# DeltaNet trunk: the triangular solve's diagonal blocks go from 16 to 32 rows, their columns dealt to four partitions

## The chip, the cores and the metric

The kernel runs on one core of one Trainium2 chip. The metric is the device time of one execution in microseconds. Three runs of the kernel before gave 3022.20, 3023.15 and 3023.69, median 3023.15. Engines are named as in the profile: PE is the matrix engine (TensorE), PEld its weight loads, DVE the vector engine, ACT the scalar engine, POOL is GpSimd, SP issues the DMAs.

## The reference, cut to what matters

The whole is a two-layer decoder trunk over 272 tokens (16 meta tokens and 256 others) of width 2048, in float32: a gated DeltaNet layer, then a differential attention layer, each followed by an MLP with squared ReLU. The change touches the DeltaNet layer alone, and in it the triangular solve of each chunk:

```python
decay = jnp.exp(jnp.where(tri_incl, G[..., :, None] - G[..., None, :], -jnp.inf))
kb = kc * bc[..., None]
a_kk = jnp.where(tri_strict, jnp.einsum('bhik,bhjk->bhij', kb, kc) * decay, 0.0)
rhs = jnp.concatenate([vc * bc[..., None], kb * jnp.exp(G)[..., None]], axis=-1)
sol = lax.linalg.triangular_solve(a_kk, rhs, left_side=True, lower=True, unit_diagonal=True)
```

For each head a unit lower triangular matrix I + A has to be applied inversely to a right-hand side; the state S is then carried from chunk to chunk.

## The kernel before, in words

The kernel works with chunks of 128, 128 and 16 tokens (`CH`), not with the reference's 64, and with 32 value heads in 8 batches of 4 (`NB`, `HB`). Nearly all of its time goes into the large products of weights and activations. A weight tile of 128x2048 is loaded by SP into `wraw` (three buffers), cut into two halves of 1024 columns, and each half is split into a rounded part `whi` (ACT, L137) and the rest `wlo` (DVE, L139), three buffers for each. `mm3` (L152, L155, L156) then issues three products for each 128x128 block: 48 for a whole tile. I call such a product of 272 columns a weight product, and half a tile (24 of them) a half-tile.

The DeltaNet layer fills the span from about 50 to 1045 us. For each batch b PE works through four tiles of keys and queries (`keys`), four of values (`values`), four of gates (`gates`) and, for batch b-2, four of the output projection (`gate_out`). The small work of the recurrence is written as Python generators. An object `flow` keeps a clock that each weight product moves on, and resumes a generator when its waiting time has run out, so that the recurrence is dealt out between the weight products. A list scheduler then sets the order on each engine; that order is fixed before the kernel runs. Three things force the flow on: a batch's `values` needs the batch before to have finished its second chunk, `keys` of batch b needs batch b-2 to be done, and `gate_out` needs the batch's own output.

For one batch the recurrence has these steps:

- `products` (from L672): the products of keys with keys and queries (`ps_u`), scaled into `UA` by DVE (L712). The diagonal blocks of `UA` are sent to DRAM (`scr`, L718), eight 16x16 blocks for each head and chunk, and POOL then clears the diagonal blocks in `UA` (`below`, L734).
- `solve` (L737 to L757): the blocks come back as `na`, one block for each partition: 2 chunks x 4 heads x 8 blocks, and 4 for the short chunk, 68 in all. `forward` (L624 to L631) inverts them all at once on DVE by forward substitution: for each row i a product of the rows so far with row i of A (L630) and a sum over them (L631), 15 rows. The inverses go through DRAM (L751, L752) into the block diagonal of `DT` (L755) and into `DT3` (L757).
- `core`, with `merge(c)` (L826 to L858) once for each of the two long chunks. From the inverses of 16-row blocks it makes those of 32-row blocks: POOL picks out the part of A that lies inside the 32-row blocks but outside the 16-row ones (`us`), DVE transposes DT (`e16`, L836), PE multiplies (`ps_e`, L840), ACT copies (`ae`, L842), PE multiplies again (`ps_d`, L846), DVE adds (`d32`, L848). Then DVE transposes the result (`dn`, L850) and PE makes NT from it (`ps_n`, L854; copied by ACT, L856). Each PE step is four products of 128x128 by 128x128 in float32, one for each head.
- `core`, chunk by chunk: from the state S come `ps_ks` and `ps_qs` (L880), from them R (DVE, L884). Three products with NT (`ps_a`, L896) with a copy by ACT (L903) or a sum by DVE (L907, L910) between them solve the rest of the triangle; a product with the inverse (`ps_w`, L916) gives w, and ACT scales it (`ws`, L922). `ps_s` (`ps_s2` in the code, L929) and S (L933, L936) carry the state on, `ps_o` (L941) gives the output, which is normed (squares L951, scaling L966) and transposed (`ps_ot`, L810). Every step waits for the one before. The outputs of `core` on PE have two PSUM banks between them (`psc`).
- `halves` (L979, L980) splits the batch's output for `gate_out`.

For the last batch (b = 7) the waits are shorter (`STEP7`), since its `core` has to be done before the last `gate_out`, the one of batch 7, can begin.

Of the kernel before, what the change touches and what calls it, by code (L numbers as in the profile page):

```python
# [10 lines left out]
F32 = mybir.dt.float32  # L11
# [6 lines left out]
P = 128  # L18
D = 2048
KT = D // P  # L20
HD = D // 2
NM = 16
SEQ = 256
L = SEQ + NM
EPS = 1e-6
# [2 lines left out]
PSM, PSC, PSK = 4, 2, 2  # L28
HB = 4
LAG = 2  # L30
G1 = 9
GB = 4
HOLD = 1
QGAP = 3.0
# [468 lines left out]
def gdn(ctx, tc, a, e):  # L503
# [24 lines left out]
    def work(name):  # L528
        return gt.tile([P, HB, P], F32, tag="g1", name=name, bufs=G1)

# [71 lines left out]
    DT = gc.tile([P, 2, HB, P], F32, name="DT")  # L602
    nc.vector.memset(DT, 0.0)
    DT3 = gc.tile([NM, HB, NM], F32, name="DT3")
    KQ3 = gc.tile([P, 2, 64], F32, name="KQ3")
    nc.vector.memset(KQ3, 0.0)

# [16 lines left out]
    def forward(na, xt):  # L624

        parts, w, n = xt.shape
        tmp = gt.tile([parts, w, n], F32, tag="fw_t", name="fw_t", bufs=1)
        for i in range(1, n):
            b = na[:, None, 0:i + 1, i].broadcast_to([parts, w, i + 1])
            nc.vector.tensor_tensor(tmp[:, :, 0:i + 1], xt[:, :, 0:i + 1], b, ALU.mult)  # L630
            nc.vector.tensor_reduce(xt[:, :, i], tmp[:, :, 0:i + 1], AX.X, ALU.add)  # L631

    def heads(t, b):
        return t[:, :, HB * b:HB * b + HB].rearrange("p c (h r) -> p c h r", r=2)
# [30 lines left out]
    def products(b, g, st):  # L665
        kq, prev = g["kq"], g["prev"]
        while not gated or prev and not prev["laid"]:
            yield 1.0
        nc.vector.tensor_scalar(st, st, 4 * EPS, None, ALU.add)
        rs = rsqrt(st.rearrange("p t c h -> p (t c h)"), "rsg", [P, 12]).rearrange("p (t c h) -> p t c h", t=2, h=2)  # L670
        rq = g["rq"] = gk.tile([P, 3, 2, 2], F32, tag="sc_rq", name="sc_rq", bufs=2)
        negc = gk.tile([P, 3, 2, 2], F32, tag="sc_nc", name="sc_nc", bufs=2)  # L672
        sup = g["sup"] = gk.tile([P, 3, 2, 2], F32, tag="sc_sup", name="sc_sup", bufs=2)
        nk = g["nk"] = gk.tile([P, 3, 2], F32, tag="sc_nk", name="sc_nk", bufs=2)
        r2 = gt.tile([P, 3, 2], F32, tag="r2", name="r2")
        nc.vector.reciprocal(r2, st[:, 0])
# [13 lines left out]
        nc.gpsimd.affine_select(gb[:NM, :, 256:L], gb[:NM, :, 256:L], pattern=[[0, HB], [1, NM]], base=0,  # L690
                                channel_multiplier=-1, compare_op=ALU.is_ge, fill=NEG)
        scr = dram.tile([2, HB, 8, NM, NM], F32, name="scr")
        scr3 = dram.tile([HB, NM, NM], F32, name="scr3")
        UA = g["UA"] = []
        for c, (o, n) in enumerate(CH):
            while prev and prev["chunk"] < min(c, 1):
                yield 1.0
            if c < 2:
                ua = gk.tile([P, HB, 2, P], F32, tag="UA", name="UA", bufs=3)
            else:  # L700
                ua = gk.tile([NM, HB, 2, NM], F32, tag="UA3", name="UA3", bufs=2)
            UA.append(ua)
            for h in range(2):
                pu = psk.tile([P, 512], F32, tag="k", name="ps_u")
                pu_v = pu[:n, 0:2 * n].rearrange("p (t i) -> p t i", t=2)
                nc.tensor.matmul(pu_v, kq[:, h, 0, o:o + n], kq[:, h, :, o:o + n], start=True, stop=True)
                for r in range(2):
                    hv = 2 * h + r
                    dec = gt.tile([P, P], F32, tag="dec", name="dec", bufs=2)
                    nc.scalar.activation(dec[:n, :n], gb[:n, hv, o:o + n], AF.Exp,  # L710
                                         bias=ngG[:n, c, HB * b + hv:HB * b + hv + 1])
                    nc.vector.scalar_tensor_tensor(ua[:, hv], pu_v, negc[:n, c, h, r:r + 1],  # L712
                                                   dec[:n, None, :n].broadcast_to([n, 2, n]), ALU.mult, ALU.mult)
                yield UGAP
            if c < 2:
                for bl in range(8):
                    q = slice(NM * bl, NM * bl + NM)
                    nc.sync.dma_start(scr[c, :, bl].rearrange("h j i -> j h i"), ua[q, :, 0, q])  # L718
                below(ua, NM)
            else:  # L720
                nc.sync.dma_start(scr3.rearrange("h j i -> j h i"), ua[:, :, 0, :])
        g["laid"] = True
        while prev and not prev["free"]:
            yield 1.0
        solve(scr, scr3)
        yield STEP7[2] if b == NB - 1 else SOLVE
        while g["values"] < HB:
            yield 1.0
        yield from core(b, g)
# [6 lines left out]

    def solve(scr, scr3):  # L737

        nb = 2 * HB * 8
        na = gt.tile([nb + HB, NM, NM], F32, tag="na", name="na", bufs=1)  # L740
        xt = gt.tile([nb + HB, NM, NM], F32, tag="xt", name="xt", bufs=1)
        diag = lambda t: t.rearrange("p j i -> p (j i)")[:, 0:NM * NM:NM + 1]
        nc.gpsimd.memset(xt, 0.0)
        nc.gpsimd.memset(diag(xt), 1.0)
        nc.sync.dma_start(na[:nb], scr.rearrange("c h b j i -> (c h b) j i"))
        nc.sync.dma_start(na[nb:], scr3)
        nc.vector.memset(diag(na), 1.0)
        forward(na, xt)
        scr2 = dram.tile([nb, NM, NM], F32, name="scr2")
        scr4 = dram.tile([HB, NM, NM], F32, name="scr4")  # L750
        nc.sync.dma_start(scr2, xt[:nb])  # L751
        nc.sync.dma_start(scr4, xt[nb:])  # L752
        for bl in range(8):
            q = slice(NM * bl, NM * bl + NM)
            nc.sync.dma_start(DT[q, :, :, q].rearrange("p c h j -> p (c h) j"),  # L755
                              scr2.rearrange("(x b) m j -> b m x j", b=8)[bl])
        nc.sync.dma_start(DT3, scr4.rearrange("h m j -> m h j"))  # L757

    def values(b, g):

# [34 lines left out]
    def core(b, g):  # L795
# [28 lines left out]
        def flat(t):  # L824
            return t.rearrange("p h j -> p (h j)")

        def merge(c):

            us = work("us")
            nc.gpsimd.affine_select(us.rearrange("p h (b i) -> p h b i", i=32),  # L830
                                    UA[c][:, :, 0, :].rearrange("p h (b i) -> p h b i", i=32),
                                    pattern=[[0, HB], [-32, 4], [0, 32]], base=0, channel_multiplier=1,
                                    compare_op=ALU.is_ge, fill=0.0)
            below(UA[c], 32)
            e16 = work("e16")
            nc.vector.transpose(flat(e16), flat(DT[:, c]))  # L836
            yield step
            _, pE = bank("ps_e")
            for hv in range(HB):
                nc.tensor.matmul(pE[:, hv], us[:, hv], e16[:, hv], start=True, stop=True)  # L840
            ae = work("ae")
            nc.scalar.copy(ae, pE)  # L842
            yield step
            _, pD = bank("ps_d")
            for hv in range(HB):
                nc.tensor.matmul(pD[:, hv], ae[:, hv], DT[:, c, hv], start=True, stop=True)  # L846
            d32 = work("d32")
            nc.vector.tensor_tensor(d32, DT[:, c], pD, ALU.add)  # L848
            dn = work("dn")
            nc.vector.transpose(flat(dn), flat(d32))  # L850
# [427 lines left out]
```

## Time and profile before

| | |
|---|---|
| profiled execution, its own time | 3024.88 us |
| its span, first to last instruction | 3023.1 us |
| median of the three runs | 3023.15 us |
| mean granted PE clock | 0.993 |
| busy over the span | PE 99%, DVE 64%, ACT 49%, POOL 7% |
| DeltaNet stretch (50 to 1045 us) | 995 us, DVE busy 715.90, ACT busy 556.67 |

The profiled execution is 1.73 us above the median, of which 1.78 lie outside the span. A row of a group of instructions gives the line, the engine, what is written from what, the shape, the count after the x, then the total busy time in us and the mean of one instruction in ns, then the time that the engine sat idle before them and what ended it. One product in float32 is recorded as two PE instructions, so that x128 stands for 64 products; digits at the end of a name are dropped (`e16` is e, `d32` is d, `ps_s2` is ps_s); records of one engine overlap, so what a matmul takes of PE is read from the distance between starts.

### The profile page before, as it was taken

What the parts mean: (1) busy time and instruction counts of PE and PEld (TensorE: products, weight loads), DVE (VectorE), ACT (ScalarE), POOL (GpSimd) and SP (SyncE); (2) the same over time, 40 slices, a digit from 0 to 9 for tenths busy, and PEclk for the clock granted to TensorE, in tenths of its full rate; (3) what the DMA queues carried; (4) which work ended last, traced back from release to release, by engine and by line L of the source; (5) the groups of instructions that cost most, each with busy time, mean ns of one, the idle gap of its engine ahead of it and who ended that gap; (6) DMA issues with size and microseconds to landing.
All of it is one profiled execution on the core that took longest, in us unless ns stands there. A gap on an engine that the chain in (4) does not pass through costs nothing. (4 is left out here: it accounts for less than half of the span.)

```text
span 3023.1 us, 57162 instructions
## 1 busy us (share of the span) xinstructions
PE 2981.0 (99%) x23747; PEld 2924.3 (97%) x23747; DVE 1943.6 (64%) x3452; ACT 1490.1 (49%) x2735; POOL 205.2 (7%) x208
## 2 busy tenths in 40 slices
PE   8999999999999899999999999999999999999998
PEld 8999999999999799999999999999999999999998
DVE  7777576776867674555555558777757555555555
ACT  4565555465555454444344434455555444444443
POOL 0100010000100220000000004300004000000001
PEclk9999999999999899999999999999999999999999
DMA  5433343434434444454544443433354555555553
GB/s 211 151 137 122 142 151 135 156 124 153 146 120 144 153 155 180 168 180 169 179 170 176 173 176 145 153 140 138 143 194 165 184 187 190 183 193 183 191 187 112
DMA packets 92468, 488.36 MB, mean 162 GB/s; under 512 B 29104, under 2 KB 32528, under 8 KB 34736
## 3 DMA queue, kind: packets, MB, share of 16 engines
q1 hardware_dynamic: 92208, 484.70, 44.6%
q8 instruction: 187, 3.06, 0.4%
q14 instruction: 73, 0.60, 0.1%
HBM read 481.41 MB, written 3.25 MB: 160 GB/s over the span
## 5 line engine op out<-in xcount | busy, mean ns | idle before, releaser
L139 DVE TENSOR_TENSOR wlo<-wraw,whi 128x1024 fp32r<-128x1024 f32 x872 | 1070.0, 1229 | 770.8 <-ACT whi L137 769.5
L137 ACT ACTIVATE whi<-wraw 128x1024 fp32r<-128x1024 f32 x890 | 940.2, 1059 | 1145.7 <-PE ps_dn L156 432.1
L152 PE MATMUL ps_dn<-yh,whi 128*128 128x272 f32 (+1 forms) x2048 | 583.2, 285 | 0.0
L152 PE MATMUL ps_up<-xh,whi 128*128 128x272 f32 (+1 forms) x2048 | 582.8, 285 | 0.0
L156 PE MATMUL ps_dn<-yl,whi 128*128 128x272 f32 (+1 forms) x2048 | 582.3, 284 | 0.0
L155 PE MATMUL ps_up<-xh,wlo 128*128 128x272 f32 (+1 forms) x2048 | 581.0, 285 | 0.2 <-DVE wlo L139 0.2
L155 PE MATMUL ps_dn<-yh,wlo 128*128 128x272 f32 (+1 forms) x2048 | 580.9, 284 | 0.0
L156 PE MATMUL ps_up<-xl,whi 128*128 128x272 f32 (+1 forms) x2048 | 580.3, 285 | 0.1
L152 PE MATMUL ps_in<-xh,whi 128*128 128x272 f32 x1520 | 460.2, 303 | 0.0
L156 PE MATMUL ps_in<-xl,whi 128*128 128x272 f32 x1520 | 441.6, 291 | 0.8 <-DVE xl L320 0.8
L155 PE MATMUL ps_in<-xh,wlo 128*128 128x272 f32 x1520 | 441.3, 291 | 0.0
L152 PEld LDWEIGHTS ps_up<-xh,whi 128*128 128x128 f32 x2048 | 385.9, 188 | 0.5 <-ACT xh L401 0.4
L155 PEld LDWEIGHTS ps_dn<-yh,wlo 128*128 128x128 f32 x2048 | 386.0, 188 | 0.0
L152 PEld LDWEIGHTS ps_dn<-yh,whi 128*128 128x128 f32 x2048 | 385.5, 188 | 0.0
L156 PEld LDWEIGHTS ps_up<-xl,whi 128*128 128x128 f32 x2048 | 384.8, 188 | 0.5 <-DVE xl L409 0.5
L155 PEld LDWEIGHTS ps_up<-xh,wlo 128*128 128x128 f32 x2048 | 384.6, 188 | 0.5 <-DVE wlo L139 0.5
L156 PEld LDWEIGHTS ps_dn<-yl,whi 128*128 128x128 f32 x2048 | 384.8, 188 | 0.0
L152 PEld LDWEIGHTS ps_in<-xh,whi 128*128 128x128 f32 x1520 | 287.2, 189 | 7.7 <-issue 4.9
L155 PEld LDWEIGHTS ps_in<-xh,wlo 128*128 128x128 f32 x1520 | 287.6, 189 | 1.6 <-issue 0.4
L156 PEld LDWEIGHTS ps_in<-xl,whi 128*128 128x128 f32 x1520 | 286.6, 189 | 1.4 <-DVE xl L320 1.0
L475 DVE TENSOR_TENSOR acc<-acc,ps_dn 128x272 f32<-128x272 f32 (+1 forms) x224 | 95.9, 428 | 122.1 <-PE ps_dn L156 121.4
L152 PE MATMUL ps_at<-xh,whi 128*128 128x272 f32 x512 | 154.5, 302 | 0.0
(313 smaller groups left out, 4476.9 us busy)
## 6 DMA issues: line engine op xcount, KB each, us to landing
wraw<-w_up SPq DMA_DIRECT2D x128, 1024.0 KB, 4.8
wraw<-w_down SPq DMA_DIRECT2D x128, 1024.0 KB, 4.8
wraw<-w_in SPq DMA_DIRECT2D x97, 1024.0 KB, 4.8
wraw<-w_out SPq DMA_DIRECT2D x32, 1024.0 KB, 4.9
wraw<-w_kv SPq DMA_DIRECT2D x32, 1024.0 KB, 4.8
wraw<-w_q SPq DMA_DIRECT2D x16, 1024.0 KB, 5.8
wraw<-w_o SPq DMA_DIRECT2D x16, 1024.0 KB, 5.6
gb<-g_dram SPq DMA_DIRECT2D x8, 544.0 KB, 5.6
```

The lines of the kernel that those rows point to most:

```text
L137: nc.scalar.activation(hi, part, AF.Copy)
L139: inst = eng.tensor_tensor(lo, part, hi.bitcast(F32), ALU.subtract)
L152: one = nc.tensor.matmul(ps, wh, rh, start=(k == 0), stop=False)
L155: nc.tensor.matmul(ps, wl, rh, start=False, stop=False)
L156: ring["mm"] = nc.tensor.matmul(ps, wh, rl, start=False, stop=(k == nk - 1))
L475: nc.vector.tensor_tensor(acc[:, m, :N], acc[:, m, :N], ps[:, :N], ALU.add)
```

## The change

- Blocks of 32 rows (`NS`) go to DRAM in place of those of 16: four DMAs for each long chunk in place of eight, and POOL clears 32-row blocks in `UA` right away.
- There are 2 x 4 x 4 = 32 such blocks. Each is loaded into four partitions, so that all 128 are used, and partition q of the four solves the columns q, q + 4, q + 8, ... of the inverse, eight of them. Since column j is zero above row j, row i works on i // 4 + 1 columns only. `xt` starts with ones on its diagonal, put there by four copies on ACT.
- The short chunk has a `forward` of its own: 4 x 16 partitions, one column each, 15 rows.
- `forward` is now a generator that yields 3.0 units of the flow's clock after each 8 rows; before, it ran in one piece.
- The inverses go back to DRAM in four DMAs, one for each q, and into `DT` in four DMAs in place of eight.
- `merge` keeps only its last part: the transpose `dn` now reads `DT` itself, then `ps_n` and NT. `us`, `e16`, `ps_e`, `ae`, `ps_d` and `d32` are gone, two of its yields too, and `ps_w` reads `DT` in place of `d32`.
- The pool of working tiles has 7 buffers in place of 9 (`G1`).

```diff
-G1 = 9
+G1 = 7
...
+    e4 = gc.tile([P, 4], F32, name="e4")
+    nc.vector.tensor_reduce(e4, ident.rearrange("p (q x) -> p q x", q=4), AX.X, ALU.add)
...
+    def forward(na, xt, w, per, name):
+
+        parts, n = na.shape[0], na.shape[1]
+        tmp = gt.tile([parts, w, n], F32, tag=name, name=name, bufs=1)
         for i in range(1, n):
-            b = na[:, None, 0:i + 1, i].broadcast_to([parts, w, i + 1])
-            nc.vector.tensor_tensor(tmp[:, :, 0:i + 1], xt[:, :, 0:i + 1], b, ALU.mult)
-            nc.vector.tensor_reduce(xt[:, :, i], tmp[:, :, 0:i + 1], AX.X, ALU.add)
+            k = min(w, i // per + 1)
+            b = na[:, None, 0:i + 1, i].broadcast_to([parts, k, i + 1])
+            nc.vector.tensor_tensor(tmp[:, :k, 0:i + 1], xt[:, :k, 0:i + 1], b, ALU.mult)
+            nc.vector.tensor_reduce(xt[:, :k, i], tmp[:, :k, 0:i + 1], AX.X, ALU.add)
+            if i % RUN == RUN - 1:
+                yield RUNGAP
...
-        solve(scr, scr3)
+        yield from solve(scr, scr3)
...
-        forward(na, xt)
-        scr2 = dram.tile([nb, NM, NM], F32, name="scr2")
-        nc.sync.dma_start(scr2, xt[:nb])
+        yield from forward(na, xt, NS // 4, 4, "fw_t")
+        scr2 = dram.tile([P // 4, NS, NS], F32, name="scr2")
+        for q, cols in enumerate(scr2.rearrange("x (s q) j -> q x s j", q=4)):
+            nc.sync.dma_start(cols, xt[P // 4 * q:P // 4 * (q + 1)])
+        yield from forward(ns, xs, 1, NM, "fw_s")
...
         def merge(c):
 
-            us = work("us")
...
-            e16 = work("e16")
-            nc.vector.transpose(flat(e16), flat(DT[:, c]))
-            yield step
-            _, pE = bank("ps_e")
-            for hv in range(HB):
-                nc.tensor.matmul(pE[:, hv], us[:, hv], e16[:, hv], start=True, stop=True)
-            ae = work("ae")
-            nc.scalar.copy(ae, pE)
-            yield step
-            _, pD = bank("ps_d")
-            for hv in range(HB):
-                nc.tensor.matmul(pD[:, hv], ae[:, hv], DT[:, c, hv], start=True, stop=True)
-            d32 = work("d32")
-            nc.vector.tensor_tensor(d32, DT[:, c], pD, ALU.add)
             dn = work("dn")
-            nc.vector.transpose(flat(dn), flat(d32))
+            nc.vector.transpose(flat(dn), flat(DT[:, c]))
             yield step
             _, pN = bank("ps_n")
             ...
-            merged[c] = d32, NT
+            merged[c] = DT[:, c], NT
```

The order on PE at the end of the DeltaNet layer, before: from batch 7's `ps_s` of its second chunk to the first product of its short chunk. The rows with `ps_out` are weight products of the output projection of batch 6; after them none is left until batch 7 is done.

```order
L929 MATMUL ps_s_12158<-ws,kn 128x256 x2
L941 MATMUL ps_o<-w,UA 128x128 x4
L152 MATMUL ps_out<-oh,whi 128x272
L155 MATMUL ps_out<-oh,wlo 128x272
L156 MATMUL ps_out<-ol,whi 128x272
...
L880 MATMUL ps_ks<-S,KQ_262 48x256 x2
L916 MATMUL ps_w<-R,DT_261 16x128 x4
```

The same place now, from the last weight product of batch 6 on.

```order
L159 MATMUL ps_out<-ol,whi 128x272
L927 MATMUL ps_s_12276<-ws,kn 128x256 x2
L939 MATMUL ps_o<-w,UA 128x128 x4
L878 MATMUL ps_ks<-S,kq 128x256 x2
L878 MATMUL ps_qs<-S,kq 128x256 x2
L894 MATMUL ps_a<-R,NT 128x128 x4
L828 MATMUL ps_ot<-ident,ov 128x128 x4
L894 MATMUL ps_a<-t_12328,NT 128x128 x4
L894 MATMUL ps_a<-z,NT 128x128 x4
L914 MATMUL ps_w<-z,DT 128x128 x4
L927 MATMUL ps_s_12361<-ws,kn 128x256 x2
L939 MATMUL ps_o<-w,UA 128x128 x4
```

What moved: the first chunk's last steps and the whole second chunk of batch 7 now come behind the last weight product of batch 6; before, only the short chunk did.

The order on DVE in the middle of a batch's forward substitution, before: one stretch from one `wlo` to the next, with `fw_t` the products of the rows.

```order
L139 TENSOR_TENSOR wlo<-wraw,whi 128x1024
L630 TENSOR_TENSOR fw_t<-xt,na 68x16x11
L792 SCALAR_TENSOR_TENSOR oT<-zt,ps_in 128x272
L631 TENSOR_REDUCE xt<-fw_t 68x16
L959 TENSOR_TENSOR o_ms<-o_ms,sc_rq 128x12
L630 TENSOR_TENSOR fw_t<-xt,na 68x16x12
L960 TENSOR_TENSOR o_ms<-o_ms,sc_rq 128x12
L631 TENSOR_REDUCE xt<-fw_t 68x16
```

The same stretch of a batch now; `fw_s` belongs to the short chunk's forward.

```order
L142 TENSOR_TENSOR wlo<-wraw,whi 128x1024
L639 TENSOR_TENSOR fw_t<-xt,na 128x4x14
L810 SCALAR_TENSOR_TENSOR oT<-zt,ps_in 128x272
L640 TENSOR_REDUCE xt<-fw_t 128x4
L640 TENSOR_REDUCE xs<-fw_s 64x1
L957 TENSOR_TENSOR o_ms<-o_ms,sc_rq 128x12
L639 TENSOR_TENSOR fw_t<-xt,na 128x4x15
L958 TENSOR_TENSOR o_ms<-o_ms,sc_rq 128x12
L639 TENSOR_TENSOR fw_s<-xs,ns 64x12
L640 TENSOR_REDUCE xt<-fw_t 128x4
L959 TENSOR_SCALAR o_ms<-o_ms 128x12
L640 TENSOR_REDUCE xs<-fw_s 64x1
```

What moved: the two forwards are interleaved, each instruction is smaller, and there are more of them. From its first row to its last, a batch's forward lies beside 5 instructions `wlo` before (7 for the last batch) and beside 9 to 13 now.

The order on PE in the second chunk of a middle batch now; before, 24 to 27 weight products stand between one `ps_a` and the next.

```order
L894 MATMUL ps_a<-R,NT 128x128 x4
L789 MATMUL ps_v<-ident,vt 128x128 x2
L789 MATMUL ps_v<-ident,vt 16x128
L155 MATMUL ps_in<-xh,whi 128x272
L158 MATMUL ps_in<-xh,wlo 128x272
L159 MATMUL ps_in<-xl,whi 128x272
...
L894 MATMUL ps_a<-t_6423,NT 128x128 x4
```

What moved: the second chunk of a middle batch is reached later and is then run through faster, with six weight products and the transposes of one value head between these two steps.

More of the change, by code (lines that the diff above doesn't have):

```diff
@@ L22 @@
 NM = 16
+NS = 32
+NBL = P // NS
+RUN, RUNGAP = 8, 3.0
 SEQ = 256
@@ L604, in gdn @@
     DT3 = gc.tile([NM, HB, NM], F32, name="DT3")
+    eye_s = gc.tile([HB * NM, NM], F32, name="eye_s")
+    e4 = gc.tile([P, 4], F32, name="e4")
+    nc.vector.tensor_reduce(e4, ident.rearrange("p (q x) -> p q x", q=4), AX.X, ALU.add)
+    nc.vector.tensor_reduce(eye_s, ident[:HB * NM, :HB * NM].rearrange("p (h j) -> p j h", j=NM), AX.X, ALU.add)
     KQ3 = gc.tile([P, 2, 64], F32, name="KQ3")
@@ L622, in conv_silu @@
         nc.vector.scalar_tensor_tensor(out, th, 1.0, ac, ALU.add, ALU.mult)
-    def forward(na, xt):
-        parts, w, n = xt.shape
-        tmp = gt.tile([parts, w, n], F32, tag="fw_t", name="fw_t", bufs=1)
+    def forward(na, xt, w, per, name):
+        parts, n = na.shape[0], na.shape[1]
+        tmp = gt.tile([parts, w, n], F32, tag=name, name=name, bufs=1)
         for i in range(1, n):
-            b = na[:, None, 0:i + 1, i].broadcast_to([parts, w, i + 1])
-            nc.vector.tensor_tensor(tmp[:, :, 0:i + 1], xt[:, :, 0:i + 1], b, ALU.mult)
-            nc.vector.tensor_reduce(xt[:, :, i], tmp[:, :, 0:i + 1], AX.X, ALU.add)
+            k = min(w, i // per + 1)
[4 more added lines that the diff above has]
+                yield RUNGAP
     def heads(t, b):
@@ L691, in products @@
                                 channel_multiplier=-1, compare_op=ALU.is_ge, fill=NEG)
-        scr = dram.tile([2, HB, 8, NM, NM], F32, name="scr")
+        scr = dram.tile([2, HB, NBL, NS, NS], F32, name="scr")
         scr3 = dram.tile([HB, NM, NM], F32, name="scr3")
@@ L715, in products @@
             if c < 2:
-                for bl in range(8):
-                    q = slice(NM * bl, NM * bl + NM)
+                for bl in range(NBL):
+                    q = slice(NS * bl, NS * bl + NS)
                     nc.sync.dma_start(scr[c, :, bl].rearrange("h j i -> j h i"), ua[q, :, 0, q])
-                below(ua, NM)
+                below(ua, NS)
             else:
@@ L737, in solve @@
     def solve(scr, scr3):
[L739 to L742, printed above, removed]
-        nc.gpsimd.memset(xt, 0.0)
[L744 to L747, printed above, removed]
@@ L748, in solve @@
-        forward(na, xt)
-        scr2 = dram.tile([nb, NM, NM], F32, name="scr2")
-        scr4 = dram.tile([HB, NM, NM], F32, name="scr4")
-        nc.sync.dma_start(scr2, xt[:nb])
-        nc.sync.dma_start(scr4, xt[nb:])
-        for bl in range(8):
-            q = slice(NM * bl, NM * bl + NM)
+        na = gt.tile([P, NS, NS], F32, tag="na", name="na", bufs=1)
+        ns = gt.tile([HB * NM, NM, NM], F32, tag="ns", name="ns", bufs=1)
+        xt = gt.tile([P, NS // 4, NS], F32, tag="xt", name="xt", bufs=1)
@@ new lines, in solve @@
+        xs = gt.tile([HB * NM, 1, NM], F32, tag="xs", name="xs", bufs=1)
+        flat = lambda t: t.rearrange("p j i -> p (j i)")
+        nc.gpsimd.memset(xt, 0.0)
+        for r in range(4):
+            nc.scalar.copy(flat(xt)[:, r:r + (NS + 4) * (NS // 4 - 1) + 1:NS + 4], e4[:, r:r + 1].broadcast_to([P, NS // 4]))
+        nc.scalar.copy(xs[:, 0], eye_s)
+        blocks = scr.rearrange("c h b j i -> (c h b) (j i)")
+        nc.sync.dma_start(flat(na), blocks[None, :, :].broadcast_to([4, P // 4, NS * NS]))
@@ new lines, in solve @@
+        nc.sync.dma_start(flat(ns), scr3.rearrange("h j i -> h (j i)")[:, None, :].broadcast_to([HB, NM, NM * NM]))
+        nc.vector.memset(flat(na)[:, 0:NS * NS:NS + 1], 1.0)
+        nc.vector.memset(flat(ns)[:, 0:NM * NM:NM + 1], 1.0)
+        yield from forward(na, xt, NS // 4, 4, "fw_t")
+        scr2 = dram.tile([P // 4, NS, NS], F32, name="scr2")
+        for q, cols in enumerate(scr2.rearrange("x (s q) j -> q x s j", q=4)):
+            nc.sync.dma_start(cols, xt[P // 4 * q:P // 4 * (q + 1)])
@@ L755, in solve @@
+        yield from forward(ns, xs, 1, NM, "fw_s")
+        scr4 = dram.tile([HB * NM, NM], F32, name="scr4")
+        nc.sync.dma_start(scr4, xs[:, 0])
+        for bl in range(NBL):
+            q = slice(NS * bl, NS * bl + NS)
             nc.sync.dma_start(DT[q, :, :, q].rearrange("p c h j -> p (c h) j"),
-                              scr2.rearrange("(x b) m j -> b m x j", b=8)[bl])
-        nc.sync.dma_start(DT3, scr4.rearrange("h m j -> m h j"))
+                              scr2.rearrange("(x b) m j -> b m x j", b=NBL)[bl])
@@ L759, in values @@
+        nc.sync.dma_start(DT3, scr4.rearrange("(h m) j -> m h j", m=NM))
     def values(b, g):
```

5 lines of the change are left out of this document (removed).

## The prediction

> **What bounds the kernel now.** I read first the page's busy times, then the windows that cut out the DeltaNet layer, the only stage that the change touches, then the waits of PE.
>
> ```profile
> PE 2981.0 (99%) x23747; PEld 2924.3 (97%) x23747; DVE 1943.6 (64%) x3452; ACT 1490.1 (49%) x2735; POOL 205.2 (7%) x208
> ```
>
> ```profile
> 50.00:1045.00 995.00, 983.31 (x7641) 949.69 (x7641) 715.90 (x1548) 556.67 (x1332) 69.83 (x82) 0.99 0.40 140
> 790.00:800.00 10.00, 10.00 (x82) 9.98 (x81) 9.93 (x32) 5.66 (x16) 0.00 (x0) 1.00 0.47 158
> 820.00:830.00 10.00, 10.00 (x82) 10.00 (x82) 6.36 (x11) 4.02 (x4) 0.00 (x0) 1.00 0.37 129
> ```
>
> The columns of the windows are the length, then the busy time of PE, PEld, DVE, ACT and POOL, then the granted clock. In the layer PE is busy for 983.31 of 995 us, DVE for 715.90. Two windows matter later: while a batch's forward substitution runs (790 to 800) DVE is busy for 9.93 of 10 us and PE still never stops; without one (820 to 830) DVE needs 6.36.
>
> ```profile
> PE ps_in L305 <- DVE xg L297: 8.4, 1, 8.4
> PE ps_ot L810 <- ACT ov L966: 6.8, 2, 5.5
> ...
> PE ps_w L916 <- ACT ps_o L951: 1.7, 1, 1.7
> ```
>
> The 8.4 us lie at the kernel's start; the two others lie at the end of the layer, where the last batch's short chunk runs with nothing beside it. So PE sets the time, and a change is worth what it takes from PE's own work, less what it opens as new gaps.
>
> **What goes from PE.** The change removes `ps_e` and `ps_d`: two groups of four float32 products for each of 16 chunk-and-batch pairs, 32 groups.
>
> ```profile
> L846 PE MATMUL ps_d<-DT,ae 128*128 128x128 f32 x128 | 16.9, 275 | 0.0
> L840 PE MATMUL ps_e<-e,us 128*128 128x128 f32 x128 | 16.9, 275 | 0.0
> ```
>
> Here is what one group takes, on PE's timeline:
>
> ```profile
> 969.74 0.29 PE L155 MATMUL ps_out<-oh,wlo 128*128 128x272 f32 x1
> 969.87 0.29 PE L156 MATMUL ps_out<-ol,whi 128*128 128x272 f32 x1
> 969.99 1.05 PE L840 MATMUL ps_e<-e,us 128*128 128x128 f32 x8
> 970.88 1.06 PE L896 MATMUL ps_a<-z,NT 128*128 128x128 f32 x8
> ```
>
> The busy sums give 33.8 us, but records overlap. From the start of `ps_e` to the next start is 0.89 us; a weight product takes 0.126 us in the same way. So 32 x 0.89 = 28.5 us leave PE's work, and this I take. PE waited 0.0 us before either group, so no wait goes with them. The ACT copies, the DVE sums and transposes and POOL's selections that go too lay beside PE's work and are worth nothing by themselves.
>
> **What DVE gets.** A forward now has 31 rows, and the short chunk's own has 15: 46 products and 46 sums for each batch in place of 15 and 15.
>
> ```profile
> L630 DVE TENSOR_TENSOR fw_t<-xt,na 68x256 f32<-68x256 f32 x8 | 4.9, 614 | 0.1
> L630 DVE TENSOR_TENSOR fw_t<-xt,na 68x112 f32<-68x112 f32 x8 | 2.8, 348 | 0.2
> L631 DVE TENSOR_REDUCE xt<-fw_t 68x16 f32<-68x256 f32 x8 | 3.3, 414 | 0.1
> L631 DVE TENSOR_REDUCE xt<-fw_t 68x16 f32<-68x112 f32 x8 | 2.1, 258 | 0.1
> ```
>
> ```profile
> L630 DVE TENSOR_TENSOR fw_t<-xt,na 68x32 f32<-68x32 f32 (+14 forms) x120 | 53.8, 448 | 2.3
> L631 DVE TENSOR_REDUCE xt<-fw_t 68x16 f32<-68x32 f32 (+14 forms) x120 | 35.5, 296 | 1.7
> L850 DVE STREAM_TRANSPOSE dn<-d 128x512 f32<-128x512 f32 x16 | 11.3, 707 | 0.3
> L836 DVE STREAM_TRANSPOSE e<-DT 128x512 f32<-128x512 f32 x16 | 11.3, 705 | 1.9 <-DMA DT<-scr 1.9
> L848 DVE TENSOR_TENSOR d<-DT,ps_d 128x512 f32<-128x512 f32 x16 | 10.9, 683 | 4.3 <-PE ps_d L846 4.0
> ```
>
> From the two sizes of each: a product of n elements takes 141 + 1.85 n ns, a sum 137 + 1.08 n. Row i works on (i // 4 + 1)(i + 1) elements, 3047 over the 31 rows; the short chunk adds 135. That makes 12.4 us of products and 9.7 of sums, 22.1 us a batch; before it was (53.8 + 35.5) / 8 = 11.2. Over 8 batches DVE gains 88 us and loses 22.2 (`e16`, `d32`): 716 + 66 = 782 us of some 980, 80%. As a mean that is no bound. Locally it is close.
>
> ```profile
> wraw<-w_in SPq DMA_DIRECT2D x97, 1024.0 KB, 4.8
> wraw<-w_out SPq DMA_DIRECT2D x32, 1024.0 KB, 4.9
> ```
>
> The layer has 97 + 32 weight tiles, so a half-tile lasts 995 / 258 = 3.86 us on average, and the order puts about 11 of them beside a forward: 42 us. In these DVE has 0.636 x 42 = 27 us of other work and 22.1 of forward: 49 us by durations, 17% too much. But the same sum before is 5 half-tiles, 19 us, against 12.1 + 11.2 = 23.3, 23% too much, and PE lost nothing, since neighbouring records overlap.
>
> What the slack is: a half-tile's `whi` can start when PE leaves the third half-tile before it, 2 x 24 x 0.126 = 6.0 us ahead of its use.
>
> ```profile
> L139 DVE TENSOR_TENSOR wlo<-wraw,whi 128x1024 fp32r<-128x1024 f32 x872 | 1070.0, 1229 | 770.8 <-ACT whi L137 769.5
> L137 ACT ACTIVATE whi<-wraw 128x1024 fp32r<-128x1024 f32 x890 | 940.2, 1059 | 1145.7 <-PE ps_dn L156 432.1
> ```
>
> Less 1.06 and 1.23 that is 3.7 us by which DVE may be late. The new waits lie there too: `dn` now waits for `DT` straight from its DMA, with the next `wlo` queued behind it on DVE and PE behind that; on SP the four stores of the inverses wait for the last sum, with loads of `wraw` behind them. Bounds for all this: 0, or 8 x (7 - 3.7) = 26 us if the 7 us of overload count in full. I take 4, near the lower end, since the heavier-booked stretch before cost nothing.
>
> The Trainium skill ("VectorE: DVE Perf Modes", section on the TRN2 errata) speaks against this part: each vector instruction pays a fixed latency, so many small ones should be avoided. The fits agree (141 and 137 ns, over half of the 22.1 us). By its 151 cycles and one element a cycle the forward would be an estimated 21 us, and the sum would not move.
>
> **What the last batch loses.** Behind batch 6's last weight product PE now has `ps_s` to `ps_o` of batch 7's two chunks, with nothing between. The steps, from these rows (ACT's, then DVE's):
>
> ```profile
> L951 ACT ACTIVATE ps_o<-ov 128x128 f32<-128x128 f32 (+1 forms) x96 | 25.9, 270 | 7.5 <-DVE ov L947 6.3
> L922 ACT ACTIVATE ws<-ps_w,sc_sup 128x128 f32<-128x128 f32 x64 | 19.0, 365 | 13.2 <-PE ps_w L916 13.2
> L951 ACT ACTIVATION_READ_ACCUMULATOR ps_o<-ov 128x1 f32 (+1 forms) x96 | 18.0, 187 | 0.0
> L903 ACT COPY t<-ps_a 128x512 f32<-128x512 f32 x16 | 9.3, 581 | 7.5 <-PE ps_a L896 7.5
> L933 ACT COPY S<-ps_s 128x512 f32<-128x512 f32 x8 | 4.7, 586 | 1.4 <-PE ps_s L929 1.4
> ```
>
> ```profile
> L910 DVE TENSOR_TENSOR z<-z,ps_a 128x512 f32<-128x512 f32 x16 | 10.9, 682 | 10.3 <-PE ps_a L896 10.3
> L884 DVE SCALAR_TENSOR_TENSOR R<-ps_ks,neG,nv 128x128 f32<-128x128 f32 x32 | 9.7, 343 | 2.2 <-PE ps_ks L880 2.2
> L936 DVE SCALAR_TENSOR_TENSOR S<-S,eGL,ps_s 128x128 f32<-128x128 f32 x32 | 9.4, 340 | 9.1 <-PE ps_s L929 9.0
> ```
>
> A group ends 1.05 us after its start. `ps_s` and the copy of S take 1.7; `ps_ks` and four R 2.4; three `ps_a`, each with a copy or a sum and some 0.1 to 0.2 for the hand-overs, 3 x 1.85; `ps_w` and four `ws` 2.4; `ps_s` and four S 2.4: 14.4 us. Two waits may come on top, both estimates: `ps_qs` needs the PSUM bank into which the first chunk's squares are written, four of 0.27 + 0.19 after the copy of `ps_o`, some 1.2 us; and `ps_ot` stands ahead of the second `ps_a`, so its norm and the four scalings come first, some 1.7. So 14.4 to 17.3 us pass, of which PE works 10 x 0.89 + 0.6 = 9.5 that it had to do anyway: 4.9 to 7.8 us of new gaps. Then the clock:
>
> ```profile
> 1004.00:1006.00 2.00, 0.30 (x2) 0.00 (x0) 1.70 (x4) 1.90 (x9) 0.00 (x0) 1.00 0.49 205
> 1006.00:1007.00 1.00, 0.95 (x7) 0.59 (x8) 0.97 (x7) 0.14 (x1) 0.00 (x0) 0.76 0.00 0
> 1007.00:1020.00 13.00, 5.49 (x19) 1.98 (x17) 4.74 (x25) 5.55 (x20) 0.00 (x0) 0.50 0.01 1
> ```
>
> At this place before, after 2 us with 0.30 us of work and the wait of 1.7 us above, PE's clock fell to half and stayed there. Half clock adds 0.89 to each step's group: 0 if it holds, 7 if it falls at once, 3 if midway. I take 7 + 3 = 10 us.
>
> **Smaller edits.** In the middle batches the second chunk runs with six weight products and one head's transposes between two `ps_a`: 0.89 + 6 x 0.126 = 1.65 us and the transposes, where a step needs 1.85. 1 us in all, from 0 to 19 (below). The five small ACT copies replace two `ae` copies; SP issues 21 DMAs a batch for 30; the broadcast load of `na` adds 0.5 MB to a batch's 16 tiles of 1 MB on DMA engines 40% busy; POOL, busy for 70 of 995 us, loses work. Fewer working tiles serve fewer users. All this lies beside PE's work: nothing, and up to 1 us if one of them is late once.
>
> **The sum.** -28.5 + 10 + 4 + 1 = -13.5 us. The profiled execution's 3024.88 (span 3023.1 and 1.8 around it) becomes 3011.4; it stood 1.7 above the median, so 3009.6 for the median.
>
> **The rivals.**
>
> *All hidden* (0.12): the last batch costs its lower bound 5, the rest nothing: 3023.15 - 23.5 = 2999.6. For it: DVE's overload cost nothing before. Against it: the order leaves the chain bare.
>
> *The clock falls at once* (0.13): the tail costs 15: 3014.6. The rule in the Trainium skill ("TensorE: Matmul & The Clock Gate", "Why this matters for your kernels") asks only that no idle gap exceed some 3 us; by it the clock would hold, the tail cost some 7 and the time be 3006.6. The trace does not agree: the clock fell after 1.7.
>
> *The middle chain is laid bare* (0.12): the flow runs batch 7's predecessors' second chunks too fast. Each step's ACT or DVE answer may find a `whi` (1.06) or `wlo` (1.23) ahead, 0.6 us on average, less 0.15 that the transposes may leave spare: 0.45 x 6 steps x 7 batches = 19 us. -28.5 + 10 + 19 = 0.5: 3023.6, no change. Against it: PE's waits before name no such step, though batch 1 had a few as close.
>
> *DVE becomes the bound, slower* (0.11): in each forward stretch `wlo` falls behind and PE stops. Between 3.3 (overload less slack) and 7 us a batch: 26 to 56, so -28.5 + 11 + 26 to 56 gives 3032 to 3062; I take 3040. It decides from (28.5 - 11) / 8 = 2.2 us a batch on.
>
> The forecast itself keeps 0.52, on its own 3004 to 3016. Something of 0.2%, 6 us, is what a measurement here can tell from none. Faster by more than that: the forecast, the first two rivals and the edge of the third, 0.78; the same 0.12; slower 0.10. The range reaches from the all-hidden case to the no-change case, 2998 to 3026.
>
> **What would show it.** Right: PE's busy time in the layer lower by some 28 us, no rows `ps_e` and `ps_d`; forward rows of 22 us a batch; waits of PE on R, t, z, ws and S only behind batch 6's last weight product, some 5 to 8 us there. Wrong: PE's weight products waiting on `wlo` (DVE bound), or on `ps_a` and `ps_w` steps between 300 and 900 us (chain bare); a PE sum that falls by much less than 28 would say that the 0.89 was mis-sized.

## The result and the profile after

The changed kernel takes 3055.08 us (median of 4 runs, 3048.75 to 3056.83) against 3023.42 for the kernel before: ratio 1.0101, 95% interval 1.0084 to 1.0119. It is slower, by 32 us, where 3009.6 was forecast. The profiled execution took 3055.07 us, its span 3053.4.

The page's line of busy times after:

```profile
PE 2972.6 (97%) x23491; PEld 2909.5 (95%) x23491; DVE 1980.0 (65%) x3926; ACT 1483.4 (49%) x2759; POOL 167.9 (6%) x168
```

PE has 256 instructions fewer but only 8.4 us less to do by its records, and DVE's mean load hardly moved. Next the DeltaNet layer, from 50 us to the first weight product of its last output projection, before and then after (columns as in the prediction's windows):

```profile
50.00:1020.10 970.10, 958.41 (x7456) 924.79 (x7455) 697.51 (x1512) 541.78 (x1306) 61.88 (x78) 0.99 0.39 138
```

```profile
50.00:1050.40 1000.40, 950.07 (x7204) 910.40 (x7202) 734.57 (x1987) 534.79 (x1331) 25.70 (x39) 0.97 0.41 140
```

The layer grew from 970.1 to 1000.4 us, all of the loss. PE stood idle in it for 970.1 - 958.4 = 11.7 us before and for 1000.4 - 950.1 = 50.3 now. PE's waits, whom it waited for and for how long (total, times, longest):

```profile
PE ps_ks L878 <- DVE S L934: 25.0, 7, 4.5
...
PE ps_a L894 <- DVE z L905: 4.7, 2, 3.9
PE ps_in L158 <- DVE ns L763: 3.6, 1, 3.6
```

The state `S`, needed by the short chunk's first product, is late in six batches, by 3.6 to 4.5 us each. The two other rows lie in the first batches: `z` (3.9) and, put down to the small memset of `ns`, a weight product with `wlo` (3.6): it starts at 108.39 us, when the `wlo` that began at 107.12 has ended. This one wait is at the place where the prediction looked for trouble on DVE; the others are not. PE's timeline at one place where `S` is late, in batch 2:

```profile
416.15 0.29 PE L158 MATMUL ps_in<-xh,wlo 128*128 128x272 f32 x1
420.62 1.91 PE L878 MATMUL ps_ks<-S,KQ 128*48 128x256 f32 x4 [4.19 <-DVE S L934]
422.46 0.60 PE L159 MATMUL ps_in<-xl,whi 128*128 128x272 f32 x1
422.86 0.43 PE L155 MATMUL ps_in<-xh,whi 128*128 128x272 f32 x1
423.09 0.43 PE L158 MATMUL ps_in<-xh,wlo 128*128 128x272 f32 x1
```

PE issues nothing for over 4 us, and then a weight product takes 0.23 us from start to start in place of 0.126. The windows of these two stretches give the granted clock (third figure from the end):

```profile
416.30:420.60 4.30, 0.14 (x2) 0.01 (x1) 3.02 (x13) 0.00 (x0) 0.00 (x0) 0.99 0.19 32
420.60:424.60 4.00, 3.98 (x15) 2.77 (x16) 2.71 (x15) 1.24 (x6) 0.00 (x0) 0.58 0.62 242
```

So each gap is paid for twice, once as a gap and once in half clock behind it. What was DVE doing? Its timeline at the same place:

```profile
409.93 0.68 DVE L908 TENSOR_TENSOR z<-z,ps_a 128x512 f32<-128x512 f32 x1
417.42 0.09 DVE L762 MEMSET na<- 128x32 f32 x1 [6.80 <-DMA na<-scr]
417.61 0.16 DVE L639 TENSOR_TENSOR fw_t<-xt,na 128x2 f32<-128x2 f32 x1
417.80 0.15 DVE L640 TENSOR_REDUCE xt<-fw_t 128x1 f32<-128x2 f32 x1
417.98 1.21 DVE L142 TENSOR_TENSOR wlo<-wraw,whi 128x1024 fp32r<-128x1024 f32 x1
...
419.37 1.11 DVE L934 SCALAR_TENSOR_TENSOR S<-S,eGL,ps_s 128x128 f32<-128x128 f32 x4
```

Nothing: for 6.8 us it stands at the memset that writes the ones on the diagonal of `na` (here that of the next batch), until the load of `na` has landed. DVE starts nothing that stands behind the memset before it. `S` stands there, though its own input was there from about 414.9 (`ps_s` started at 413.70 and takes 1.2). The load, on SP:

```profile
407.79 0.58 SPq L760 DMA_DIRECT2D na<-scr  x1
```

From its issue at 407.79 to the memset at 417.42 pass 9.6 us. Before, the load was of 64 KB; the view of its line ends thus:

```profile
DMA to landing us min/median/max: 3.4/3.4/3.4
```

It has 512 KB now, but size alone doesn't explain it, since a weight tile of 1 MB landed in 4.8. The DMA view of 409.5 to 414.5 us, when only this load is under way, says what does:

```profile
DMA packets 93, 0.38 MB, mean 76 GB/s; under 512 B 0, under 2 KB 0, under 8 KB 93
## 3 DMA queue, kind: packets, MB, share of 16 engines
q1 hardware_dynamic: 93, 0.38, 23.6%
```

The load keeps 23.6% of 16 engines busy, as much as 3.8 of them, and the trace's records of single packets have exactly four under way for 90% of this stretch. Its outermost step counts the four copies. The wait recurs in seven of eight batches (DVE's waits in the layer):

```profile
DVE na L762 <- DMA na<-scr: 47.3, 7, 7.9
```

The order on DVE has its part in this. Before, DVE ran the memset 7.3 to 9.3 us after the issue of the load in seven of eight batches, behind other work; now it is ready for it 2.8 to 3.4 us after the issue in six of them. A late load costs DVE time only where DVE comes to it early.

### The profile page after: what moved, and what is told of

Same layout as the page of the kernel before. It is cut to its first block, busy times and chain, and to the rows that moved or that the text cites. A ratio compares the mean times of both kernels' runs of the same rounds, so it can differ in the third digit from the quotient of the medians.

```text
span 3053.4 us, 56970 instructions
## 1 busy us (share of the span) xinstructions
PE 2972.6 (97%) x23491; PEld 2909.5 (95%) x23491; DVE 1980.0 (65%) x3926; ACT 1483.4 (49%) x2759; POOL 167.9 (6%) x168
```

## The experiments

Theory A: the load of `na` runs on four DMA engines and lands late; DVE stands in front of it with `S` queued behind; PE stops. Theory B: the forward's many small instructions on DVE make `S` late (the prediction's own rival). The time of the kernel before beside these runs was 3024.04, 3024.77 or 3023.32 us; each ratio is to that of its own chip.

### fold: the same load, laid so that its outermost step counts 32

```diff
-    nc.vector.tensor_reduce(e4, ident.rearrange("p (q x) -> p q x", q=4), AX.X, ALU.add)
+    nc.vector.tensor_reduce(e4, ident.rearrange("p (x q) -> p q x", q=4), AX.X, ALU.add)
...
-        nc.sync.dma_start(flat(na), blocks[None, :, :].broadcast_to([4, P // 4, NS * NS]))
+        nc.sync.dma_start(flat(na), blocks[:, None, :].broadcast_to([P // 4, 4, NS * NS]))
...
-            nc.sync.dma_start(cols, xt[P // 4 * q:P // 4 * (q + 1)])
+            nc.sync.dma_start(cols, xt[q:P:4])
```

> The changed kernel; only the way in which the 32 blocks are laid over the partitions differs: partition 4x+q (not 32q+x) holds block x and the columns q, q+4, ..., so that the outermost step of the four-fold load of na counts 32 blocks and no longer 4 copies. Same bytes, same number of DMAs, the same rows in the same order on PE, DVE and SP. Theory A (late load: the load of na runs on four of the 16 DMA engines, 82 GB/s at a busy share of 25%, and lands 9.6 us after its issue; DVE, which works strictly in order, stands 6.8 us at the memset of na with S queued behind, and PE stops some 4.3 us a batch for S and then runs at half clock): the load is spread, lands within 5 us, DVE waits under 2 us a batch in that place, PE's waits on S fall from 25 us to under 6, and the time falls from 3055 by 25 to 45 us to 3010 to 3030. Theory B (overload: the 23 us a batch of small forward steps on DVE make S late, whatever the load does): 3050 to 3057, PE's waits on S over 18 us.

Measured: 3005.21 us (3003.95 to 3007.12), ratio 0.994, 0.9924 to 0.9957: 50 us less than the changed kernel, and less than the kernel before. SP's and DVE's rows at the same place of batch 2:

```profile
385.98 0.56 SPq L760 DMA_DIRECT2D na<-scr  x1
```

```profile
388.00 0.68 DVE L908 TENSOR_TENSOR z<-z,ps_a 128x512 f32<-128x512 f32 x1
390.75 0.09 DVE L762 MEMSET na<- 128x32 f32 x1 [2.06 <-DMA na<-scr]
...
391.50 1.23 DVE L142 TENSOR_TENSOR wlo<-wraw,whi 128x1024 fp32r<-128x1024 f32 x1 [0.19 <-ACT whi L140]
...
393.03 1.12 DVE L934 SCALAR_TENSOR_TENSOR S<-S,eGL,ps_s 128x128 f32<-128x128 f32 x4
```

From issue to memset it is 4.8 us now, not 9.6; DVE waits 2.06, not 6.80; and `S` starts 5.0 us behind `z` where it was 9.4. The 128 packets of the load pass in 3.0 us, where the changed kernel's took 7.6. `S` still stands behind the memset, and PE's waits for it are down from 25.0 us to 0.4 in all:

```profile
PE ps_ks L878 <- DVE S L934: 0.4, 1, 0.4
```

The layer's window:

```profile
50.00:998.50 948.50, 931.86 (x7198) 895.55 (x7197) 735.10 (x1985) 534.49 (x1327) 26.66 (x39) 0.99 0.43 147
```

It is 51.9 us shorter than that of the changed kernel, and the two figures say in what: idle 948.5 - 931.9 = 16.6 in place of 50.3, 33.7 us; and the same products take 931.86 in place of 950.07, 18.2 us, which is half clock (0.97 granted there, 0.99 here). The expected 25 to 45 us had counted the waits and little of the clock, and 3005 lies below its 3010 to 3030. Theory B falls as the cause of the loss: PE's rows come in the same order in both traces, and so do DVE's but for a few neighbours that change places.

### spread: four loads in place of one

```diff
-        nc.sync.dma_start(flat(na), blocks[None, :, :].broadcast_to([4, P // 4, NS * NS]))
+        for q in range(4):
+            nc.sync.dma_start(flat(na)[P // 4 * q:P // 4 * (q + 1)], blocks)
```

> The changed kernel with its own layout over the partitions; the load of na is cut into four DMAs, one for each group of 32 partitions, 128 KB each with an outermost count of 32. Another way to the same end as the run fold: if the number of DMA engines is what made the load late, the busy share of the DMA engines during it is over twice the 25% of the changed kernel and the time is near fold's, 3002 to 3010 (three more issues of some 0.6 us on SP; the scheduler also puts S ahead of the memset). If it was the layout over the partitions or the order of reading in DRAM that fold mended, and not the spread: 3040 to 3057.

Measured: 3003.33 us (3002.6 to 3006.26), ratio 0.9936, 0.9921 to 0.9951. The DMA view of 387.5 to 391.5 us, while the four loads are under way (beside the end of one load and the start of another):

```profile
q1 hardware_dynamic: 328, 0.82, 70.8%
```

They landed in 4.4 us (median, 3.2 to 5.2). The layout over the partitions is that of the changed kernel here, so what makes the load late is neither the layout nor the order of reading, but the number of DMA engines. The time of this run can't show as much: the scheduler put `S` ahead of the memset, which DVE starts at 398.12 us, 11 us after the first of these loads was issued (387.08). The changed kernel's slow load was waited for until 9.6 us after its issue at the place shown, so it too would hardly have been late here.

### dummy: the slow load, put into the kernel before

```diff
+        xx = gt.tile([P, 4 * NM * NM], F32, tag="xx", name="xx", bufs=1)
+        for i in range(2):
+            nc.sync.dma_start(xx[64 * i:64 * i + 64],
+                              scr.rearrange("c h (b k) j i -> (c h b) (k j i)", k=4)[None, :, :]
+                              .broadcast_to([4, 16, 4 * NM * NM]))
         nc.sync.dma_start(na[:nb], scr.rearrange("c h b j i -> (c h b) j i"))
```

> The kernel before with 7 working buffers, computing all that it did; ahead of the load of na stand two more loads that nothing reads, 256 KB each, as four copies of 16 rows of 4 KB (outermost count 4): in sum the bytes and the shape of the changed kernel's load. Theory A: these 512 KB go over four DMA engines, na lands 6 to 8 us later behind them, DVE stands at its memset for 4 to 7 us a batch, and PE stops where wlo or S is queued behind: 3 us of slack cover part, so 1 to 4 us a batch with its half clock: 3030 to 3060. Theory B (the forward's work on DVE is what costs, the load nothing): 3020 to 3027.

Measured: 3033.65 us (3032.0 to 3034.13), ratio 1.0031, 1.0019 to 1.0043. DVE's waits between 150 and 1003 us, which before have no such row:

```profile
DVE na L750 <- DMA na<-scr: 13.5, 6, 3.9
```

The time is 9.6 us longer with DVE's instructions the same in kind and number, at the low end of A's span: DVE came to the memset later than in the changed kernel, and stood 2 to 4 us there, not 6 to 8. But this run is weak evidence for A. PE has no wait for `S` in it; the new waits are one each for `e16` (2.0 us), w (1.3) and the scaled output (2.3). The edit also took the working buffers from 9 to 7 and changed the order on PE and DVE, and what these cost by themselves was not measured.

### delay: the memset moved away from the load

```diff
+        yield 12.0
         nc.vector.memset(flat(na)[:, 0:NS * NS:NS + 1], 1.0)
```

> The changed kernel with its slow load of na as it is; the generator of solve only waits 12 units of the flow's clock (some 13 us) between the loads and the two memsets, so that the memset and the forward come later in DVE's order. Theory A (late load in front of DVE's queue): the load has landed when DVE comes to the memset, DVE's wait there falls from 41 us in the middle of the layer to under 10, PE's waits on S to under 6, and the middle of the layer gains 25 to 45 us; but batch 7's inverses come 13 us later, so that its first chunk too falls behind the last weight product of batch 6, 7 steps more with about 1 us of gap each and half clock, 10 to 16 us: 3020 to 3046. Theory B (overload): nothing gained in the middle, the same loss at the end: 3063 to 3075.

Measured: 3073.92 us (3067.11 to 3080.55), ratio 1.0165, 1.0146 to 1.0184. The number is the one written down for theory B, but the trace shows that the edit didn't do what it was meant to do. DVE at the place (the load was issued at 412.88):

```profile
415.53 0.69 DVE L909 TENSOR_TENSOR z<-z,ps_a 128x512 f32<-128x512 f32 x1 [1.25 <-PE ps_a L895]
424.21 0.09 DVE L763 MEMSET na<- 128x32 f32 x1 [8.00 <-DMA na<-scr]
...
426.07 0.86 DVE L935 SCALAR_TENSOR_TENSOR S<-S,eGL,ps_s 128x128 f32<-128x128 f32 x3
```

The scheduler put the memset right behind `z` and ahead of `S` as before, and the load is no earlier. DVE waits 8.0 us, and PE's waits on `S` are longer:

```profile
PE ps_ks L879 <- DVE S L935: 38.2, 7, 7.4
```

So it tells nothing for B; a longer wait at this place goes with a slower kernel, though 13.2 us more of waits on `S` are not the whole of the 19 by which it is slower, and more of batch 7 is bare at the layer's end too. A slow load with `S` ahead of the memset was not tried by itself.

### nomerge: only the removal from PE

```diff
-            nc.vector.transpose(flat(dn), flat(d32))
+            nc.vector.transpose(flat(dn), flat(DT[:, c]))
...
-            merged[c] = d32, NT
+            merged[c] = DT[:, c], NT
```

with the lines from `us` to `d32` taken out of `merge`.

> The kernel before with its 16-row blocks and its DVE forward; the merging of the 16-row inverses is left out (us, e, ps_e, ae, ps_d, d), and NT and w are made from the inverses of 16-row blocks as they stand, so that a part of the computation is missing. This is the half of the change that takes work from PE, alone. If the term of the sum is right (32 groups of 0.89 us on PE's path, nothing else bound by it): 28.5 us less for the products; 60 weight products now stand behind batch 7's short chunk, so the gaps at the layer's end (6.8 + 1.7 us of waits and some 10 us of half clock) may go too: 3023 - 28.5 = 2994.5, down to 2980. If the products lay beside other waiting: 3010 to 3023.

Measured: 2990.24 us (2985.84 to 2991.94), ratio 0.9886, 0.9872 to 0.9901: 33.8 us less, between the two figures expected for a term of the right size. The layer (up to the same event):

```profile
50.00:984.40 934.40, 925.46 (x7203) 894.04 (x7201) 679.18 (x1480) 531.24 (x1290) 34.42 (x46) 1.00 0.41 144
```

### nofwd and twice: what the forward costs on DVE

nofwd, on fold:

```diff
-            nc.vector.tensor_tensor(tmp[:, :k, 0:i + 1], xt[:, :k, 0:i + 1], b, ALU.mult)
-            nc.vector.tensor_reduce(xt[:, :k, i], tmp[:, :k, 0:i + 1], AX.X, ALU.add)
+            if i < 2:
+                nc.vector.tensor_tensor(tmp[:, :k, 0:i + 1], xt[:, :k, 0:i + 1], b, ALU.mult)
+            if i < 2:
+                nc.vector.tensor_reduce(xt[:, :k, i], tmp[:, :k, 0:i + 1], AX.X, ALU.add)
```

> The kernel of the run fold (the load of na spread over the DMA engines), in which forward issues only its first row; the products and sums of rows 2 and up are left out, so the inverses are not solved and a part of the computation is missing. All yields, loads and stores stay, and PE's order of the end of the layer is the same. Some 22 us a batch of small instructions leave DVE. If the forward's work on DVE still costs PE time (the 4 us of the prediction, or the overload of the rival): 3.5 to 26 us less than fold's 3005.2, so 2979 to 3001.7. If DVE takes the forward in its stride once the load is early: 3003 to 3007.

Measured: 2999.42 us (2999.15 to 2999.74), ratio 0.9917, 0.9902 to 0.9932. That is 5.8 us under fold by the medians, 7 by the ratios (the two ran on different chips), and the two profiled executions differ by 4.2. The ratios' intervals overlap a little (fold's begins at 0.9924): by them anything from about nothing to some 14 us is possible, and the sign is likely rather than certain.

twice, on fold:

```diff
             nc.vector.tensor_tensor(tmp[:, :k, 0:i + 1], xt[:, :k, 0:i + 1], b, ALU.mult)
+            nc.vector.tensor_tensor(tmp[:, :k, 0:i + 1], xt[:, :k, 0:i + 1], b, ALU.mult)
```

> The kernel of the run fold with each product of the forward issued twice into the same place: the same values, some 13 us a batch more of small DVE instructions (23 to 36). If DVE had room (no bound near): 3005 to 3010, and some 2 to 6 us more for batch 7, whose inverses come later. If DVE was at its bound in the forward's stretches: at least 8 x (13 - 4) = 70 us more, 3075 and up; in between, the part that is not hidden shows how much room was left.

Measured: 3028.0 us (3025.65 to 3032.92), ratio 1.0014, 1.0004 to 1.0023. Some 103 us more of DVE work in the whole cost 23 us over fold: neither free nor a bound, about a fifth shows. PE then waits a little in many places, the longest in total for the keys:

```profile
PE ps_kn L661 <- DVE kq L630: 8.0, 7, 3.0
```

### fold7_20, fold7_15, fold7_10: the last batch earlier

```diff
-STEP7 = (2.0, 5.0, 35.0)
+STEP7 = (2.0, 5.0, 20.0)
```

and with 15.0 and 10.0, on fold.

> The kernel of the run fold with one number changed: the last batch's recurrence may begin 20 units of the flow's clock after its forward, not 35, so that its second chunk again stands between weight products of batch 6; only the last state product, the short chunk and what follows stay behind them. If the end's term is right (4.9 to 7.8 us of gaps and some 3 of half clock lie in the second chunk's bare steps): 6 to 11 us less than fold's 3005.2: 2994 to 2999. If the inverses now come too late for the earlier steps (they go through DRAM): 3000 to 3010, with PE waiting for NT or dn.

Measured: 2999.45 us (2996.75 to 2999.57), ratio 0.9915, 0.99 to 0.993: 5.8 us under fold by the medians, 0.5 us above the range expected. (These three runs were on another chip than fold; by the ratios they lie 7.6, 11.2 and 9.4 us under it.)

> As the run before with 15 units: nearly the whole of batch 7's recurrence stands between weight products, and only the short chunk's turned output with its norm comes last. If the end's term is right: the short chunk's bare steps (1.9 + 1.7 us and the small ones, with half clock, 5 to 8 us) are hidden as well: 2987 to 2994. If the inverses come too late: above 2999.

Measured: 2995.09 us (2993.53 to 2997.39), ratio 0.9903, 0.9888 to 0.9918: 10.1 us under fold, 1 us short of what was expected. The layer:

```profile
50.00:989.80 939.80, 930.20 (x7196) 894.74 (x7194) 733.87 (x1983) 533.05 (x1325) 25.61 (x39) 1.00 0.43 148
```

Idle PE time is 9.6 us, less than the 11.7 of the kernel before.

> As the run fold7_15 with 10 units. The second chunk is no earlier in PE's order than with 15, so no more is won there: 2993 to 2998. If the inverses of batch 7 are now too late, PE waits for NT or dn there: 2998 to 3010.

Measured: 2994.9 us (2992.55 to 2997.11), ratio 0.9909, 0.9892 to 0.9925. As expected nothing more, and no wait for the inverses. With the load spread and the last batch earlier, the change gives about 1%; the kernel before was not given an earlier last batch, so part of this may be had without the change.

## Why the prediction was wrong, point by point

**The step that failed** is in the smaller edits: "the broadcast load of na adds 0.5 MB to a batch's 16 tiles of 1 MB on DMA engines 40% busy", put at nothing. It compared bytes with the mean load of all engines. The load uses a quarter of the engines, and what DVE meets is the time until this one load has landed, not the mean share. The prediction listed DVE's new waits (`dn` on `DT`) and SP's, and overlooked the one at the head of `solve`, which stood in the kernel before too, but later in DVE's order and behind a load of 3.4 us. fold prices the step at 50 us, in the layer's windows 34 of idle PE and 18 of half clock.

The Trainium skill had the rule that would have shown it ("DMA: Bandwidth & Descriptors", section "Why a DMA increments its semaphore by 16 and not by 1"): a DMA runs on the largest number of engines up to 16 that divides the slowest step's count on both sides. By it 4 and 128 give 4 engines, 32 and 128 give 16. The traces agree, with 23.6% of 16 engines in the changed kernel against 70.8% in spread, whose loads count 32 on both sides.

**The products taken from PE**, 28.5 us, were sized well. nomerge gave 33.8, with 60 weight products now behind the last short chunk, so that a part of the end's old gaps went too. From before to fold PE's own time in the layer fell by 958.41 - 931.86 = 26.6 us. In the changed kernel itself this is hidden, since half clock lengthens the products that are left.

**The forward** was put at 22.1 us a batch. Its rows after:

```profile
L639 DVE TENSOR_TENSOR fw_t<-xt,na 128x2 f32<-128x2 f32 (+30 forms) x248 | 84.4, 340 | 2.5
L640 DVE TENSOR_REDUCE xt<-fw_t 128x1 f32<-128x2 f32 (+30 forms) x248 | 62.5, 252 | 1.6
...
L639 DVE TENSOR_TENSOR fw_s<-xs,ns 64x2 f32<-64x2 f32 (+14 forms) x120 | 19.0, 158 | 0.0
...
L640 DVE TENSOR_REDUCE xs<-fw_s 64x1 f32<-64x2 f32 (+14 forms) x120 | 17.5, 146 | 0.0
```

Together 183.4, 22.9 a batch. Its price on PE, taken as 4 us, came out at 4 to 7 (nofwd), with the wide margin given there. Of `wlo` waits, the place that the rival "DVE becomes the bound" gave to the loss, there was the one of 3.6 us, behind the late memset. That rival had the sign and, with 3032 to 3062, the time, but by luck: its mechanism, too much DVE work, was not what happened, as fold shows with the same work. What came late stood behind a memset that waited for a load.

**The last batch's end** was put at 7 us of gaps and 3 of half clock. The gaps came as worked out: in fold seven of 0.58 to 1.71 and one of 0.16, 7.1 us (from start to start, less what the products take; the idle time that a timeline prints is a little less). The clock did not fall in them; a window of the changed kernel from the middle of them, and the one in which it falls:

```profile
1027.00:1032.00 5.00, 2.94 (x19) 2.34 (x19) 1.20 (x2) 1.30 (x5) 0.00 (x0) 1.00 0.00 0
1032.00:1036.00 4.00, 2.57 (x15) 1.57 (x14) 3.11 (x12) 1.37 (x7) 0.00 (x0) 1.00 0.00 0
1036.00:1044.00 8.00, 4.87 (x20) 1.88 (x20) 3.41 (x17) 2.98 (x10) 0.00 (x0) 0.65 0.00 1
```

It held at 1.00 and fell only at the short chunk's waits, where it fell before. So the end cost some 7 and not 10, and the rival "the clock falls at once" is refuted. The prediction had set this case's one wait of 1.7 us against the rule in the Trainium skill ("TensorE: Matmul & The Clock Gate", "Why this matters for your kernels") on gaps over some 3 us; for these gaps of about 1 us the rule was the better guide. It is not the whole of it, since waits of under 2 us did halve the clock elsewhere (last section).

**The middle chain laid bare**: refuted. Between 300 and 925 us PE's waits in fold are 0.2 us in all, and in the changed kernel 16.0 of 16.5 are on `S`.

**The sum** without the failed step: -28.5 + 7.1 + 6 = -15.4. fold measures -18.8 (3005.21 against 3024.04; by its interval -13 to -23). So the rest of the working stands, and its own -13.5 lies just inside. What the sum had at nothing turned the sign.

## What to carry to other kernels

A transfer that grows is to be priced by its time to landing on the engines that it really uses, read from the busy share while it alone is under way; a broadcast whose outermost step counts the copies uses few. Ask of each first use of loaded data what stands behind it on that engine's queue: a cheap memset that waits for a late load holds up everything after it. Where a change fails, keep the order of instructions and change one suspected transfer: here three edited lines turned a loss of 1.0% into a gain of 0.6%.

## What the runs showed of the hardware

A gap in PE's work of 3.7 us or more (3.73, 3.76, 4.06 and five from 4.2 to 4.6 in the changed kernel, from start to start) was each time followed by a granted clock of 0.50 to 0.69 over the next 4 us, while the gaps of up to 1.71 us behind batch 6's last weight product, with PE busy for 2.94 of 5 us, left it at 1.00. In the layer this half clock was worth 18 us, over half of what the gaps themselves cost. Shorter gaps are not safe for that. In the kernel before, one wait of 1.9 us (`ps_kn` on `kq`, until 121.29 us) was followed by half clock too, with PE busy for 1.64 of 3.5 us (columns as in the other windows):

```profile
119.00:122.50 3.50, 1.64 (x14) 1.40 (x13) 3.40 (x7) 1.30 (x5) 0.00 (x0) 0.99 0.87 316
122.50:126.00 3.50, 3.50 (x18) 3.50 (x17) 1.78 (x3) 1.50 (x6) 2.46 (x4) 0.52 0.10 15
```

These runs do not settle where between the two the clock turns.

The load whose outermost step counted 4 ran on about four engines: 512 KB in 4 copies moved at 76 GB/s on 3.8 engines, some 20 GB/s each.
